# Residual updates and low halves of activations by adding transfers, in a two-layer diffusion step on one Trainium2 core

## The chip, the core and the metric

The kernel runs on one core of one Trainium2 chip. The time is that of the device, in microseconds, for one execution; shown is the median of three runs. Five engines work beside each other, each on its own list of instructions in a fixed order: TensorE (PE in the profile; its weight loads are PEld), VectorE (DVE), ScalarE (ACT), GpSimd (POOL) and SyncE (SP), which here only issues transfers. Data lie in SBUF (128 partitions); products come out in PSUM.

## What is computed

One inference step of a diffusion backbone of two layers. There are 640 tokens: 128 of context and 512 latent ones, which share all weights and differ in their condition vector. Everything is single precision. Cut to what matters:

```python
def swiglu(h, w_in, w_out):                      # w_in 1024 x 5632, w_out 2816 x 1024
    g, u = jnp.split(h @ w_in, 2, axis=-1)
    return (jax.nn.silu(g) * u) @ w_out

def layer(x, cond, p, lam_init, ropes, ctx):
    mods = (jax.nn.silu(cond) @ p['w_ada'] + p['b_ada']).reshape(cond.shape[0], N_MOD, 1, D_MODEL)
    sh1, sc1, g1, sh2, sc2, g2, sh3, sc3, g3 = [mods[:, i] for i in range(N_MOD)]
    h = modulate(rmsnorm(x, p['norm_ffn1']), sh1, sc1)
    x = x + 0.5 * g1 * swiglu(h, p['w_ffn1_in'], p['w_ffn1_out'])
    h = modulate(rmsnorm(x, p['norm_mix']), sh2, sc2)
    y, kv = token_mix(h, p, lam_init, ropes, ctx)
    x = x + g2 * y
    h = modulate(rmsnorm(x, p['norm_ffn2']), sh3, sc3)
    x = x + 0.5 * g3 * swiglu(h, p['w_ffn2_in'], p['w_ffn2_out'])
    return x, kv
```

`token_mix` projects to 2304 columns and mixes in four head groups (pooling, a short convolution, two kinds of attention); its exponentials are those of the attention's softmax.

## The kernel before, in words

**Layout.** Channels lie on the partitions, tokens on the free axis. `x[0]` to `x[7]`, each 128 x 640, hold the residual stream in SBUF for the whole program. Weights are streamed from HBM by SP (`load_raw`, L149) into `raw`, a ring of three buffers of 512 KB that all weights and the ada rows share.

**Single precision from a shorter format.** TensorE's fast format for four-byte numbers (fp32r) keeps fewer bits than single precision. So every operand is held as two: a high half (a copy that rounds, on ScalarE) and a low half (the number less its high half, on VectorE). For weights that is `Weights.piece` (ScalarE `hi` L165, VectorE `lo` L166, 512 columns at a time), for activations `split` (ScalarE L187, VectorE L188). Each product then takes three matmuls: high by high, high by low, low by high.

**Stages.** Two layers of FFN, token mixing, FFN: four FFNs in all. The last FFN has a tail of its own (`last_out`), which also norms and stores the output. A trace of TensorE shows FFN one from 0 to 549 us, mixing to 884, FFN two to 1374, FFN three from 1386 to 1844, mixing to 2166, FFN four to the end.

**An FFN** walks its hidden layer of 2816 in 22 column blocks of 128, in five parts of 5, 5, 4, 4 and 4 blocks (`PARTS`). A part has two stretches:

- The *pair stretch*: `pair(i)` makes gate and up of one block, by a scheme of seven products on the two halves of the tokens in place of eight. It sums weights on VectorE (`f` and `raw`, L602), splits seven pieces of weights, and issues 7 x 12 = 84 matmuls of 322 columns (`product`, L497) into the PSUM banks F, H and S, which ScalarE (L608 and the like) and VectorE take out into `t` tiles. `activation` (L538) then does SiLU on ScalarE, the multiplication on VectorE (L544), and the split (L187, L188).
- The *out stretch*: `out(k0, k1, d, ...)` for eight `d` multiplies the part's activations with the weights of the output (`mm3`, L134; 30 matmuls for a part of five blocks, 24 for one of four) into one of two buffers S, and `x_update_joined` (L518) adds the result, times the gate, to `x[d]`: two VectorE instructions (context columns and latent columns, L522) that read PSUM and `x[d]` and write `x[d]`.

**The ada products.** `mods` of the stages to come are worked out beside the FFNs by the pump: a step (`ada_steps`, L254 to L268) loads 512 KB of `w_ada` into `raw` and multiplies it with two rows on VectorE (`dump`, L264, 128 x 1024 each, with a running sum). `tick` in `activation` and `out` lets the pump go on at a rate for each FFN; in the last FFN there is none. The shift copies `sh` that POOL makes from them are at L375.

**Order and buffers.** The tile framework schedules each engine's instructions into one list from the order of the program and the buffers; there are 38 buffers in ring U (tag "U"; 128 x 644; normed inputs, halves of activations, and in mixing the exponentials `e`), 5 in ring T (`t`), 32 small ones (`s`), 3 in ring F (`f`, in mixing `kx`, which POOL clears at L995). GpSimd makes some low halves in mixing (L166) and small clears; in the FFNs it has nearly nothing to do.

Of the kernel before, what the change touches and what calls it, by code (L numbers as in the profile page):

```python
# [10 lines left out]
F32 = mybir.dt.float32  # L11
# [23 lines left out]
FFN = 2816  # L35
NP = 22
PARTS = ((0, 5), (5, 10), (10, 14), (14, 18), (18, 22))
UB = 38
RAWB = 3
HLB = 4  # L40
NPLAIN = 2
# [40 lines left out]
def hybrid_step(ctx: ExitStack, tc: tile.TileContext, x_in, cc_in, cb_in, w_ada0, w_ada, pv_in, lam_in, w_fin, w_fout, w_min, w_mout,  # L82
# [5 lines left out]
    const = ctx.enter_context(tc.tile_pool(name="const", bufs=1))  # L88
    wp = ctx.enter_context(tc.tile_pool(name="wp", bufs=2))
    up = ctx.enter_context(tc.tile_pool(name="up", bufs=UB))  # L90
    tp = ctx.enter_context(tc.tile_pool(name="tp", bufs=5))
    sp = ctx.enter_context(tc.tile_pool(name="sp", bufs=32))
    psS = ctx.enter_context(tc.tile_pool(name="psS", bufs=2, space=bass.MemoryType.PSUM))
    psH = ctx.enter_context(tc.tile_pool(name="psH", bufs=2, space=bass.MemoryType.PSUM))
    psF = ctx.enter_context(tc.tile_pool(name="psF", bufs=2, space=bass.MemoryType.PSUM))
# [4 lines left out]
    def nm(s):  # L100
        uid[0] += 1
        return f"{s}_{uid[0]}"

    def U(dt=F32R):
        return up.tile([128, UW], dt, tag="U", name=nm("u"))
# [2 lines left out]
        return tp.tile([128, UW], dt, tag="t", name=nm("t"))  # L108

    def E(dt=F32):  # L110
        return up.tile([128, UW], dt, tag="U", name=nm("e"))

    def PT():
        t = up.tile([128, 1024], F32R, tag="P", name=nm("p"), bufs=3)
# [71 lines left out]
    def split(dst_hi, dst_lo, src):  # L186
        S.activation(dst_hi, src, AF.Copy)  # L187
        V.tensor_tensor(out=dst_lo, in0=src, in1=dst_hi, op=ALU.subtract)  # L188
# [329 lines left out]
    def x_update_joined(d, p, gate):  # L518
        g = gate[d // 4]
        w = p.rearrange("p a b -> p (a b)")[:, 512 - HN:512 - HN + N]  # L520
        for c, a, b in SEGS:
            V.scalar_tensor_tensor(out=x[d][:, a:b], in0=w[:, a:b], scalar=g[:, d % 4, c:c + 1], in1=x[d][:, a:b],  # L522
                                   op0=ALU.mult, op1=ALU.add)


    def ffn(l, sub, norm, nxt, pump, prate):
        wi = w_fin[l * 2 + (0 if sub == 0 else 1)]
# [10 lines left out]
        def activation(i, g, u, cb):  # L538

            lb = HW + HN  # L540
            for a, b, c in ((0, NC, cb), (NC, lb, lb)):
                S.activation(g[:, a:b], g[:, a:b], AF.Silu, bias=g[:, c:c + 1])  # L542
            for a, b, c in ((0, NC, cb), (NC, lb, lb)):
                V.scalar_tensor_tensor(out=u[:, a:b], in0=u[:, a:b], scalar=u[:, c:c + 1], in1=g[:, a:b],  # L544
                                       op0=ALU.add, op1=ALU.mult)
            hi, lo = U(), U()
            split(*[t[:, :N].rearrange("p (h n) -> p h n", h=2) for t in (hi, lo)], FastNorm.view(u)[:, :, :HN])
            acts[i] = (hi, lo)
            tick(2.0)

# [88 lines left out]
        def out(k0, k1, d, gate, nx):  # L639
            ps = PS()  # L640
            w = load_w(wo[d, :, k0 * 128:k1 * 128], (k1 - k0) * 128)
            mm3(joined(ps), CN, w, acts[k0:k1], range(k1 - k0))
            x_update_joined(d, ps, gate)
            if nx is not None:
                nx.tile(d)
            tick(1.0)
# [907 lines left out]
```

## Time and profile before

| what | value |
|---|---|
| time, median of 3 runs | 2618.66 us (2615.48 to 2620.7) |
| profiled execution | 2611.82 us |
| its span, first to last instruction | 2610.0 us |
| its mean granted TensorE clock | 0.962 of full speed |
| TensorE / VectorE / ScalarE / POOL busy | 92% / 81% / 46% / 12% of the span |
| moved | 280.63 MB, mean 108 GB/s |

The busy shares are means over the whole program; stages differ. A row of windows gives, all in us where nothing else is said, in this order: the stretch (from:to) and its length; how long PE, PEld, DVE, ACT and POOL were busy, each with its count of instructions in brackets; the clock that TensorE was granted (1.00 is 2.4 GHz, 0.5 is 1.2 GHz); the mean busy share of the sixteen transfer engines; and GB/s. Start times in a timeline overlap a little: an instruction's duration runs to its last write, and the next one starts before that. What one costs its queue is the distance from its start to the start of the next.

### The profile page before, as it was taken

The page shows a single profiled execution, that of the slowest core. Times are in us where ns is not written, and L with a number is a line of the kernel's source. Part 1 is how long each engine was busy: PE and PEld are TensorE (multiplying, and loading weights), DVE is VectorE, ACT ScalarE, POOL GpSimd, SP SyncE. Part 2 cuts the span into 40 slices and gives each one's busy share as a digit, 9 for nine tenths or more (in the row PEclk, how much of TensorE's full clock was granted, in tenths as well). Part 3 has the DMA queues.
Part 4 walks back from the last instruction along what each step waited for, and adds up shares of the span by engine and source line. Part 5 has one row for each costly group of instructions (what it writes and reads, how often), then busy time and mean ns, then how long its engine had stood idle before and what let it go on. Part 6 is the DMA issues. An engine that isn't in the chain of part 4 may idle for free.

```text
span 2610.0 us, 41459 instructions
## 1 busy us (share of the span) xinstructions
PE 2402.5 (92%) x15497; PEld 2318.7 (89%) x15497; DVE 2127.1 (81%) x3978; ACT 1207.9 (46%) x2447; POOL 311.8 (12%) x373
## 2 busy tenths in 40 slices
PE   7798998999788798999998999999998889999998
PEld 4798988998788798988998999999988789999997
DVE  5999998767675899999789898988677768668776
ACT  4533333566554533333355343335575556344444
POOL 3100000034132200000021000001332230000002
PEclk8899999999899899999998999999998999999999
DMA  7254443222412144444322434433233112222223
GB/s 255 92 157 126 149 146 121 77 82 99 146 57 72 61 145 130 154 130 144 96 66 90 137 114 132 134 98 94 71 115 117 58 56 64 89 75 77 77 89 106
DMA packets 100553, 280.63 MB, mean 108 GB/s; under 512 B 10624, under 2 KB 18688, under 8 KB 100352
## 3 DMA queue, kind: packets, MB, share of 16 engines
q1 hardware_dynamic: 100352, 277.99, 33.4%
q8 instruction: 122, 2.00, 0.3%
q14 instruction: 79, 0.65, 0.1%
HBM read 263.00 MB, written 14.94 MB: 106 GB/s over the span
## 4 chain that ended last, share of the span: by engine, by line
PE 56%; DVE 26%; DMA 6%; ACT 6%; issue 4%; POOL 2%; SPq 0%; DVEq 0%; ACTq 0%; POOLq 0%
PE S L134 22%; PE F L497 16%; PE S L497 8%; PE F L134 5%; DVE dump L264 4%; DVE lo L166 4%; PE H L497 3%; DVE u L188 3%; DMA raw<-in_w_ada_dram 2%; DMA raw<-in_w_fin_dram 2%; DVE f L602 2%; PE H L134 2%; ACT hi L165 1%; DVE t L544 1%; DMA u<-qd 1%
## 5 line engine op out<-in xcount | busy, mean ns | idle before, releaser
L134 PE MATMUL S<-u,hi 128*128 128x320 f32 (+3 forms) x3552 | 693.6, 314 | 35.0 <-DVE x L511 16.0
L497 PE MATMUL F<-u,hi 128*128 128x322 f32 x2752 | 643.9, 321 | 57.1 <-ACT hi L165 53.3
L165 ACT ACTIVATE hi<-raw 128x512 fp32r<-128x512 f32 (+2 forms) x696 | 405.2, 594 | 600.9 <-PE S L134 244.9
L134 PEld LDWEIGHTS S<-u,hi 128*128 128x128 f32 x3552 | 566.6, 190 | 49.2 <-issue 18.5
L497 PEld LDWEIGHTS F<-u,hi 128*128 128x128 f32 x2752 | 476.3, 195 | 69.1 <-ACT hi L165 60.9
L166 DVE TENSOR_TENSOR lo<-raw,hi 128x512 fp32r<-128x512 f32 x616 | 392.2, 649 | 82.3 <-ACT hi L165 77.7
L497 PE MATMUL F<-u,lo 128*128 128x322 f32 x1376 | 439.3, 319 | 16.5 <-DVE lo L166 16.4
L134 PE MATMUL S<-u,lo 128*128 128x320 f32 (+3 forms) x1776 | 420.3, 312 | 8.0 <-DVE lo L166 8.0
L264 DVE SCALAR_TENSOR_TENSOR dump<-raw,sc 128x1024 f32<-128x1024 f32 x262 | 321.5, 1231 | 21.5 <-DMA raw<-in_w_ada_dram 17.6
L497 PE MATMUL S<-u,hi 128*128 128x322 f32 x1376 | 323.0, 321 | 7.8 <-DVE t L565 7.8
L134 PEld LDWEIGHTS S<-u,lo 128*128 128x128 f32 x1776 | 303.4, 190 | 10.5 <-DVE lo L166 9.8
L165 ACT ACTIVATE hi<-f 128x512 fp32r<-128x512 f32 x258 | 158.4, 628 | 303.1 <-PE F L497 161.6
L497 PEld LDWEIGHTS F<-u,lo 128*128 128x128 f32 x1376 | 270.9, 197 | 23.1 <-DVE lo L166 22.0
L134 PE MATMUL F<-u,hi 128*128 128x320 f32 (+1 forms) x1056 | 244.7, 321 | 10.0 <-DVE t L762 6.4
L497 PEld LDWEIGHTS S<-u,hi 128*128 128x128 f32 x1376 | 238.7, 195 | 13.0 <-ACT t L608 8.0
L497 PE MATMUL S<-u,lo 128*128 128x322 f32 x688 | 217.4, 316 | 0.0
L166 DVE TENSOR_TENSOR lo<-f,hi 128x512 fp32r<-128x512 f32 x258 | 174.8, 687 | 36.4 <-ACT hi L165 33.9
L522 DVE SCALAR_TENSOR_TENSOR x<-S,gate,x 128x128 f32<-128x128 f32 (+1 forms) x304 | 152.8, 544 | 50.6 <-PE S L134 50.2
L134 PEld LDWEIGHTS F<-u,hi 128*128 128x128 f32 x1056 | 180.5, 194 | 11.9 <-DVE t L762 6.9
L542 ACT ACTIVATE t<-t 128x128 f32<-128x128 f32 (+1 forms) x176 | 98.4, 560 | 140.3 <-DVE t L634 126.9
L134 PE MATMUL F<-u,lo 128*128 128x320 f32 (+1 forms) x528 | 158.6, 318 | 0.0
L497 PE MATMUL H<-u,hi 128*128 128x322 f32 x688 | 156.8, 313 | 1.9 <-ACT hi L165 1.9
(232 smaller groups left out, 3215.9 us busy)
## 6 DMA issues: line engine op xcount, KB each, us to landing
raw<-in_w_fin_dram SPq DMA_DIRECT2D x176, 512.0 KB
raw<-in_w_ada_dram SPq DMA_DIRECT2D x131, 512.0 KB
raw<-in_w_fout_dram SPq DMA_DIRECT2D x104, 256.0 KB
raw<-in_w_fout_dram SPq DMA_DIRECT2D x64, 320.0 KB
raw<-in_w_min_dram SPq DMA_DIRECT2D x36, 512.0 KB
u<-in_w_ada_dram SPq DMA_DIRECT2D x24, 256.0 KB
KS<-kd SPq DMA_DIRECT2D x16, 384.0 KB
raw<-in_w_mout_dram SPq DMA_DIRECT2D x16, 384.0 KB
```

What stands on the lines that cost most here:

```text
L134: PE.matmul(out, lhsT, rhs, start=start, stop=stop)
L165: S.activation(hi[:, :n], src, AF.Copy)
L166: (eng or V).tensor_tensor(out=lo[:, :n], in0=src, in1=hi[:, :n], op=ALU.subtract)
L188: V.tensor_tensor(out=dst_lo, in0=src, in1=dst_hi, op=ALU.subtract)
L264: V.scalar_tensor_tensor(out=dump[:, :D], in0=raw, scalar=1.0, in1=rows[i], op0=ALU.mult, op1=ALU.mult, accum_out=m[0][:, b, i:i + 1])
L497: PE.matmul(ps, w_, a, start=start and k == 0 and p == 0, stop=k == 3 and p == 2, skip_group_check=True)
L522: V.scalar_tensor_tensor(out=x[d][:, a:b], in0=w[:, a:b], scalar=g[:, d % 4, c:c + 1], in1=x[d][:, a:b], op0=ALU.mult, op1=ALU.add)
L542: S.activation(g[:, a:b], g[:, a:b], AF.Silu, bias=g[:, c:c + 1])
L544: V.scalar_tensor_tensor(out=u[:, a:b], in0=u[:, a:b], scalar=u[:, c:c + 1], in1=g[:, a:b], op0=ALU.add, op1=ALU.mult)
L602: V.tensor_tensor(out=o, in0=a, in1=b, op=ALU.add)
```

## The change

`x_update_joined` is replaced by `x_update_dma` in `out` for all parts but the last of each FFN: four parts of eight updates in four FFNs, 128 in all. ScalarE copies the PSUM result, times the gate, into a `t` tile (two instructions), and GpSimd's queue issues a transfer that adds the tile to `x[d]`. The low half of an activation is made by a transfer as well, for all blocks but the last of each part (17 of 22 in an FFN, 68 in all): ScalarE writes the negated high half into `lo`, and a transfer adds the number itself. The exponentials of mixing get a ring of five buffers ("e") of their own, which the low halves use in the FFNs; ring U goes from 38 to 33, ring T from 5 to 6, the small ones from 32 to 16.

```diff
--- before.py
+++ after.py
@@ -35,7 +35,9 @@
 FFN = 2816
 NP = 22
 PARTS = ((0, 5), (5, 10), (10, 14), (14, 18), (18, 22))
-UB = 38
+UB = 33
+EB = 5
+TB = 6
 RAWB = 3
 HLB = 4
 NPLAIN = 2
@@ -88,8 +90,8 @@
     const = ctx.enter_context(tc.tile_pool(name="const", bufs=1))
     wp = ctx.enter_context(tc.tile_pool(name="wp", bufs=2))
     up = ctx.enter_context(tc.tile_pool(name="up", bufs=UB))
-    tp = ctx.enter_context(tc.tile_pool(name="tp", bufs=5))
-    sp = ctx.enter_context(tc.tile_pool(name="sp", bufs=32))
+    tp = ctx.enter_context(tc.tile_pool(name="tp", bufs=TB))
+    sp = ctx.enter_context(tc.tile_pool(name="sp", bufs=16))
     psS = ctx.enter_context(tc.tile_pool(name="psS", bufs=2, space=bass.MemoryType.PSUM))
     psH = ctx.enter_context(tc.tile_pool(name="psH", bufs=2, space=bass.MemoryType.PSUM))
     psF = ctx.enter_context(tc.tile_pool(name="psF", bufs=2, space=bass.MemoryType.PSUM))
@@ -108,7 +110,7 @@
         return tp.tile([128, UW], dt, tag="t", name=nm("t"))
 
     def E(dt=F32):
-        return up.tile([128, UW], dt, tag="U", name=nm("e"))
+        return up.tile([128, UW], dt, tag="e", name=nm("e"), bufs=EB)
 
     def PT():
         t = up.tile([128, 1024], F32R, tag="P", name=nm("p"), bufs=3)
@@ -522,6 +524,15 @@
             V.scalar_tensor_tensor(out=x[d][:, a:b], in0=w[:, a:b], scalar=g[:, d % 4, c:c + 1], in1=x[d][:, a:b],
                                    op0=ALU.mult, op1=ALU.add)
 
+    def x_update_dma(d, p, gate):
+
+        g = gate[d // 4]
+        w = p.rearrange("p a b -> p (a b)")[:, 512 - HN:512 - HN + N]
+        t = T()
+        for c, a, b in SEGS:
+            S.activation(t[:, a:b], w[:, a:b], AF.Copy, scale=g[:, d % 4, c:c + 1])
+        G.dma_start(x[d], t[:, :N], accum_op=ALU.add)
+
 
     def ffn(l, sub, norm, nxt, pump, prate):
         wi = w_fin[l * 2 + (0 if sub == 0 else 1)]
@@ -543,8 +554,14 @@
             for a, b, c in ((0, NC, cb), (NC, lb, lb)):
                 V.scalar_tensor_tensor(out=u[:, a:b], in0=u[:, a:b], scalar=u[:, c:c + 1], in1=g[:, a:b],
                                        op0=ALU.add, op1=ALU.mult)
-            hi, lo = U(), U()
-            split(*[t[:, :N].rearrange("p (h n) -> p h n", h=2) for t in (hi, lo)], FastNorm.view(u)[:, :, :HN])
+            hi, lo = U(), E(F32R)
+            a = FastNorm.view(u)[:, :, :HN]
+            if i + 1 in [k1 for _, k1 in PARTS]:
+                split(*[t[:, :N].rearrange("p (h n) -> p h n", h=2) for t in (hi, lo)], a)
+            else:
+                S.activation(hi[:, :N].rearrange("p (h n) -> p h n", h=2), a, AF.Copy)
+                S.activation(lo[:, :N], hi[:, :N], AF.Copy, scale=-1.0)
+                G.dma_start(lo[:, :N].bitcast(F32).rearrange("p (h n) -> p h n", h=2), a, accum_op=ALU.add)
             acts[i] = (hi, lo)
             tick(2.0)
 
@@ -640,7 +657,7 @@
             ps = PS()
             w = load_w(wo[d, :, k0 * 128:k1 * 128], (k1 - k0) * 128)
             mm3(joined(ps), CN, w, acts[k0:k1], range(k1 - k0))
-            x_update_joined(d, ps, gate)
+            (x_update_dma if k1 < NP else x_update_joined)(d, ps, gate)
             if nx is not None:
                 nx.tile(d)
             tick(1.0)
```

The scheduler places everything anew. In the rows below a line number of the kernel after is up to 17 above that of before for the same code (weight halves L166 become L168, the sums L602 become L619, ada products L264 become L266); L533 is a gate copy of `x_update_dma` and L534 its transfer, L564 the transfer of a low half.

VectorE, first FFN, end of the out stretch of part two and start of the next pair stretch. `x_88` is updated last; `f` and `raw` are sums of weights, `dump` is an ada product. Before:

```order
L522 SCALAR_TENSOR_TENSOR x_84<-S_2689,gate_1254,x_84 128x128
L522 SCALAR_TENSOR_TENSOR x_84<-S_2689,gate_1254,x_84 128x512
L166 TENSOR_TENSOR lo_2811<-raw_2781,hi_2810 128x512
L602 TENSOR_TENSOR f_2786<-raw_2781,raw_2783 128x512
L264 SCALAR_TENSOR_TENSOR dump_2929,mod_2926<-raw_2927,sc_315 128x1024
L602 TENSOR_TENSOR raw_2783<-raw_2783 128x512
L264 SCALAR_TENSOR_TENSOR dump_2929,mod_2926<-raw_2927,sc_318 128x1024
L522 SCALAR_TENSOR_TENSOR x_88<-S_2738,gate_1256,x_88 128x128
L522 SCALAR_TENSOR_TENSOR x_88<-S_2738,gate_1256,x_88 128x512
L602 TENSOR_TENSOR f_2785<-raw_2783,raw_2781 128x512
L602 TENSOR_TENSOR f_2787<-f_2785,raw_2781 128x512
L166 TENSOR_TENSOR lo_2831<-f_2785,hi_2830 128x512
```

After:

```order
L619 TENSOR_TENSOR f_2826<-raw_2821,raw_2823 128x512
L619 TENSOR_TENSOR raw_2823<-raw_2823 128x512
L619 TENSOR_TENSOR f_2825<-raw_2823,raw_2821 128x512
L168 TENSOR_TENSOR lo_2834<-raw_2821,hi_2833 128x512
L619 TENSOR_TENSOR f_2827<-f_2825,raw_2821 128x512
L168 TENSOR_TENSOR lo_2851<-raw_2821,hi_2850 128x512
L266 SCALAR_TENSOR_TENSOR dump_2970,mod_2967<-raw_2968,sc_315 128x1024
L266 SCALAR_TENSOR_TENSOR dump_2970,mod_2967<-raw_2968,sc_318 128x1024
L168 TENSOR_TENSOR lo_2871<-f_2825,hi_2870 128x512
L266 SCALAR_TENSOR_TENSOR dump_2975,mod_2967<-raw_2973,sc_315 128x1024
L168 TENSOR_TENSOR lo_2888<-f_2826,hi_2887 128x512
```

The last two updates of `x` stood between the weight sums before; now no update is there, and the four sums come close together, ahead of the ada products.

ScalarE at the same place; `t_2791` and `t_2831` take the first product out of bank F, a `t` from `S` and a gate is a copy of an x update. Before:

```order
L165 ACTIVATE hi_2793<-raw_2781 128x512
L165 ACTIVATE hi_2810<-raw_2781 128x512
L608 ACTIVATE t_2791<-F_2788 128x322
L165 ACTIVATE hi_2830<-f_2785 128x512
L165 ACTIVATE hi_2847<-f_2786 128x512
L165 ACTIVATE hi_2865<-raw_2783 128x512
L165 ACTIVATE hi_2882<-raw_2783 128x512
L165 ACTIVATE hi_2899<-f_2787 128x512
```

After:

```order
L167 ACTIVATE hi_2833<-raw_2821 128x512
L167 ACTIVATE hi_2850<-raw_2821 128x512
L533 ACTIVATE t_2766<-S_2725,gate_1258 128x128
L533 ACTIVATE t_2766<-S_2725,gate_1258 128x512
L167 ACTIVATE hi_2870<-f_2825 128x512
L167 ACTIVATE hi_2887<-f_2826 128x512
L533 ACTIVATE t_2817<-S_2776,gate_1260 128x128
L533 ACTIVATE t_2817<-S_2776,gate_1260 128x512
L167 ACTIVATE hi_2905<-raw_2823 128x512
L625 ACTIVATE t_2831<-F_2828 128x322
L167 ACTIVATE hi_2922<-raw_2823 128x512
L167 ACTIVATE hi_2939<-f_2827 128x512
```

Four gate copies of the last two updates stand between the high halves of the first pair's weights, and the copy out of bank F comes after two more halves and two gate copies.

POOL, first FFN, around the last part. Before, with the shift copies of the next stages:

```order
L375 COPY sh_8876<-mod_4148 128x4x2
L376 COPY sh_8876<-mod_4148 128x4
L377 COPY sh_8876<-mod_4148 128x4
L995 MEMSET kx_5570 64x128
L995 MEMSET kx_5571 64x128
L349 MEMSET R_5683 128x2
L330 COPY u_5196<-shc_5202 128x2
```

After:

```order
L534 DMA x_88<-t_4653 128x640
L564 DMA e_4799<-t_4668 128x2x320
L564 DMA e_4945<-t_4814 128x2x320
L1012 MEMSET kx_5651 64x128
L1012 MEMSET kx_5652 64x128
L564 DMA e_5091<-t_4960 128x2x320
L351 MEMSET R_5764 128x2
L332 COPY u_5277<-shc_5283 128x2
```

The clears of `kx` stood behind shift copies; now transfers stand ahead of them and one low half of the last part stands behind them.

## Rows read from the trace of the kernel before

**Rows 1.** The page, part 1: busy time, share of the span, instructions, per engine.

```profile
PE 2402.5 (92%) x15497; PEld 2318.7 (89%) x15497; DVE 2127.1 (81%) x3978; ACT 1207.9 (46%) x2447; POOL 311.8 (12%) x373
```

**Rows 2.** Windows: a pair stretch and an out stretch, last FFN.

```profile
2258.00:2321.00 63.00, 63.00 (x422) 62.54 (x421) 54.25 (x95) 33.83 (x63) 0.00 (x0) 1.00 0.24 75
2321.00:2357.00 36.00, 35.85 (x245) 35.59 (x245) 19.36 (x39) 9.60 (x19) 0.00 (x0) 1.00 0.32 94
```

**Rows 3.** Windows: four of the eleven pair stretches of FFNs one to three.

```profile
170.00:245.00 75.00, 67.38 (x419) 65.80 (x418) 69.43 (x129) 32.40 (x64) 0.00 (x0) 0.93 0.35 111
283.00:338.00 55.00, 51.05 (x335) 49.45 (x334) 54.57 (x99) 25.46 (x49) 0.00 (x0) 1.00 0.38 120
370.00:437.00 67.00, 57.25 (x339) 55.58 (x339) 61.24 (x110) 27.13 (x52) 1.48 (x9) 0.90 0.36 117
...
1592.00:1646.00 54.00, 51.93 (x343) 50.68 (x342) 52.48 (x97) 25.82 (x49) 1.86 (x6) 1.00 0.37 119
```

**Rows 4.** Windows: four out stretches of FFNs one and two.

```profile
245.00:283.00 38.00, 36.41 (x243) 35.41 (x242) 34.54 (x70) 8.64 (x19) 0.00 (x0) 1.00 0.58 184
338.00:370.00 32.00, 29.42 (x194) 28.26 (x194) 29.49 (x58) 6.53 (x11) 0.00 (x0) 1.00 0.60 192
1064.00:1102.00 38.00, 36.67 (x245) 35.69 (x244) 34.46 (x71) 8.44 (x18) 1.00 (x3) 1.00 0.59 184
1159.00:1191.00 32.00, 29.49 (x194) 28.32 (x194) 29.69 (x59) 6.71 (x11) 0.00 (x0) 1.00 0.61 193
```

**Rows 5.** Waits: who waited for whom, us in total, times, longest us.

```profile
ACT hi L165 <- DVE f L602: 69.2, 28, 5.3
...
PE F L497 <- ACT hi L165: 53.3, 23, 3.8
...
PE F L497 <- DVE lo L166: 16.4, 14, 1.6
```

**Rows 6.** Timeline of VectorE: start us, us, engine, line, operation, tiles.

```profile
290.05 1.22 DVE L264 SCALAR_TENSOR_TENSOR dump<-raw,sc 128x1024 f32<-128x1024 f32 x1
291.20 0.08 DVE L264 DVE_READ_ACCUMULATOR dump<-raw,sc 128x1 f32 x1
...
391.13 0.82 DVE L188 TENSOR_TENSOR u<-t,u 128x640 fp32r<-128x640 f32 x1
391.87 0.68 DVE L602 TENSOR_TENSOR f<-raw,raw 128x512 f32<-128x512 f32 x1
```

**Rows 7.** Timeline of VectorE: the last x update of part two, first FFN.

```profile
283.62 1.00 DVE L522 SCALAR_TENSOR_TENSOR x<-S,gate,x 128x128 f32<-128x128 f32 x2
284.54 0.68 DVE L602 TENSOR_TENSOR f<-raw,raw 128x512 f32<-128x512 f32 x1
```

**Rows 8.** Groups by form, ScalarE: count | busy, mean ns | idle before, releasers.

```profile
L187 ACT ACTIVATE u<-t 128x640 fp32r<-128x640 f32 x88 | 64.9, 737 | 27.4 <-DVE t L544 27.1
...
L187 ACT ACTIVATE p<-S 128x512 fp32r<-128x512 f32 x64 | 38.2, 597 | 46.2 <-PE H L134 29.8 <-DVE p L188 12.9 <-PE S L946 2.5
```

**Rows 9.** Waits of POOL.

```profile
POOL sh L375 <- DVE mod L267: 777.8, 6, 315.5
...
POOL kx L995 <- DVE lo L166: 153.8, 4, 82.8
```

**Rows 10.** Timeline: two weight loads issued by SP's queue, and ScalarE after them.

```profile
338.65 2.07 SPq L151 DMA_DIRECT2D raw<-in_w_fout_dram  x2
...
342.12 0.63 ACT L165 ACTIVATE hi<-raw 128x512 fp32r<-128x512 f32 x1 [2.27 <-DMA raw<-in_w_fout_dram]
```

**Rows 11.** The page, part 3: the loads' queue: packets, MB, share of sixteen engines.

```profile
q1 hardware_dynamic: 100352, 277.99, 33.4%
```

**Rows 12.** Groups by form: operations with two SBUF operands, VectorE and POOL.

```profile
L264 DVE SCALAR_TENSOR_TENSOR dump<-raw,sc 128x1024 f32<-128x1024 f32 x262 | 321.5, 1231 | 21.5 <-DMA raw<-in_w_ada_dram 17.6 <-ACT sc L247 2.6
...
L166 POOL TENSOR_TENSOR lo<-raw,hi 128x512 fp32r<-128x512 f32 x64 | 87.8, 1374 | 271.2 <-ACT hi L165 238.8 <-ACT e L1196 20.2 <-ACT e L937 6.1
...
L322 DVE SCALAR_TENSOR_TENSOR u<-x,scl,u 128x512 fp32r<-128x512 f32 x16 | 24.0, 1500 | 9.2 <-ACT u L321 9.2
```

## Prediction

> **What bounds the kernel now.** I read the page first. TensorE is busy for 2402.5 of 2610 us and VectorE for 2127.1 [rows 1], so TensorE looks like the limit; but both figures are means over stages with different limits. So I cut the span into the stretches of the program. An FFN is five parts, and a part is a *pair stretch* (4 or 5 column blocks of the hidden layer, 84 matmuls each) and an *out stretch* (8 output blocks of 30 or 24 matmuls).
>
> The last FFN has no ada products, and there TensorE is full: a pair stretch does 422 matmuls in 63.0 us and an out stretch 245 in 36.0 us [rows 2]. That is 0.149 and 0.147 us a matmul, and serves as the yardstick. VectorE is busy there for 54.25 of 63 us.
>
> The same stretches of the first three FFNs are longer [rows 3]. The pair stretch at 370 us does 339 matmuls in 67.0 us where the yardstick gives 50.6: 16.4 us lost. VectorE lists 61.24 us of work, and the granted clock falls to 0.90, which it does where TensorE has stood still. Eleven such stretches lose between 2.8 us (the one at 1592) and 16.4 us, 101 us in all. Four out stretches lose 2.0 to 3.5 us, 11.3 us together [rows 4]; VectorE is busy there for 29.49 of 32.0 us or 34.54 of 38. The waits of TensorE name ScalarE's weight halves (53.3 us) and VectorE's (16.4 us) [rows 5], and ScalarE's halves wait for sums that VectorE makes. So in the first three FFNs VectorE's queue sets the end of a pair stretch; the ada products (1.15 us each, from the start to the read of its sum [rows 6]) are what fills it.
>
> **The change part by part.** Durations come from the profiled execution (2611.82 us, its span 2610.0); the median of the three runs shown is 2618.66, 6.84 us more.
>
> *Low halves.* 17 of 22 per FFN leave VectorE. One takes 0.74 us from its start to the next start [rows 6]. Only where VectorE is the limit does that count: 4 in each of the parts with five blocks, 3 in those with four. That is 3.0 or 2.2 us a stretch.
>
> *x updates.* 32 per FFN leave VectorE, 0.92 us each (two instructions, 283.62 to 284.54 [rows 7]). In an out stretch TensorE sets the pace, so most of it is hidden. Two things are not. The four out stretches of [rows 4] are short of VectorE by at most 3.5 us and get 8 x 0.92 = 7.4 us back: all 11.3 us go. And the last update of a part waits for the last matmul of its out stretch, with the first sums of the next pair stretch queued behind it (the row at 284.54 is such a sum). In the order as printed above nothing of VectorE's stands between them any more: 0.92 us for each pair stretch that follows such an out stretch.
>
> *Ada products.* Without the work above, the scheduler puts the products elsewhere. Counted in VectorE's order, pair stretches two, three and four of the first FFN hold 15, 12 and 13 of them before and 14, 10 and 11 now. In the second FFN stretches one to four go 15 to 16, 15 to 14, 12 to 10 and 13 to 11; in the third FFN only the second changes, 9 to 8. Each that moves to an out stretch is worth 1.15 us [rows 6].
>
> *Sum over the pair stretches*, in order of time and never more than a stretch loses. First FFN: 3.0 + 1.15 + 0.92 = 5.1; 2.2 + 2.3 + 0.92 = 5.4, held at its loss of 5.0 (the stretch at 283 [rows 3]); 5.4. Second: 3.0 - 1.15 = 1.8 (the mixing before it keeps its updates on VectorE); 5.1; 5.4; 5.4. Third: 3.0; 5.1; 2.8 (held); 3.1. Together 47.2, and 3.0 for the first stretch of the program, which is short of VectorE too: 50.2 us. With the out stretches 61.5 us.
>
> *What it costs.* ScalarE gets a negating copy per low half (nearest row 737 ns) and two copies per x update (nearest 597 ns from PSUM for the long one [rows 8]). In the stretch at 370 ScalarE works 27.13 of 67 us [rows 3]. If idle time covers all, it costs nothing; if each of the 38 negating copies in the eleven stretches delays a weight half, 28 us. I take 5, since a copy can delay a half only in the few places where TensorE already waits for ScalarE (23 waits [rows 5]). At the start of a pair stretch the last update's two copies stand between weight halves (second order above); the next evacuation of bank F then comes after five instructions of ScalarE and before the third product, which starts 24 x 0.149 = 3.6 us in; I put it at nothing. Cover gone, it costs some 0.5 us a stretch.
>
> POOL issues 196 transfers, and is a queue: in the last part of the FFNs before a mixing, the third low half stands behind two clears of `kx` (third order above), and `kx` waits up to 82.8 us for VectorE [rows 9]. They are released within the last pair, so this half may start only near the end of the pair stretch and is wanted 14 matmuls, 2.1 us, into the out stretch. Nearest landing: a 256 KB load issued by 340.72 lets ScalarE go on at 342.12, some 1.4 us [rows 10]. Between 0 and 4 us in each of two places; I take 1 each. The other low halves have a pair (84 x 0.149 = 12.5 us) to land. POOL's copies of ada shifts, which wait up to 315.5 us for VectorE [rows 9], stand ahead of some adds too; in VectorE's new order what they wait for is done within the same pair stretch as before, so I price that at nothing.
>
> Transfer engines: the loads take 33.4% of 2610 us for 277.99 MB [rows 11], 3.1 us of all sixteen per MB. An added transfer of 0.328 MB is then 1.03 us if it costs one copy, and up to 3.1 if it costs three. I take one copy: in the fullest out stretch (share 0.60 of 32 us [rows 4]) 19.2 + 8.2 = 27.4 us, less than TensorE's 28.5. It is hidden.
>
> Mixing: the exponentials' own five buffers change TensorE's order of scores and projections a little and VectorE's work not at all. I take 0, between -10 and +10. The last FFN gains nothing: TensorE is full there.
>
> Net 61.5 - 5 - 2 = 54.5 us: 2557 us for an execution like the profiled one, **2564 us** for the median.
>
> **The rivals.**
> *All of the loss goes.* A stretch with VectorE at 0.95 also pays for the half clock behind each stop. If VectorE's slack ends the stops altogether, the 101 + 11.3 us go and about 5 of cost stay: 2512 us. For it: the loss at 370 is three times what I credit. Against it: my counts leave 2 to 7 us more VectorE work in four of the stretches than TensorE needs.
>
> *The transfer engines fill up in the out stretches.* If an add must read the old value as well, it costs two copies, 2.06 us. Then the two stretches with four blocks and ada loads need 19.2 + 16.5 = 35.7 against 28.5 us, and four with five blocks 22.4 + 16.5 = 38.9 against 36 (share 0.59 of 38 [rows 4]): at most 26 us back, 2590 us. For it: the share of 0.60. Against: the updates have a whole part to land, and can spill into the pair stretch with its share of 0.36.
> The Trainium skill, "Collectives: The Full Stack", section "The bandwidth ceiling: the fold count and why AG ≠ RS ≠ AR", says of adds done by the DMA engines that they read two sources and so push twice the read traffic. By that rule this rival's 2.06 us would be the price; no row here shows an adding transfer.
>
> *Slower: issuing on POOL holds VectorE.* VectorE's operations with two operands in SBUF stretch when POOL works beside them: 1500 ns for 512 columns against 1231 ns for 1024 [rows 12]. If the issue of a transfer holds VectorE for h, a low half gains 0.74 - h and an update 0.92 - h. At h = 0.85 nothing is left; that is the point from which it decides. At the 1374 ns of a POOL subtraction [rows 12] the 38 low halves add 24 us and six full out stretches 6 x 8 x (1.374 - 0.92) = 22, less 11.5 for the moved products, plus 7: +41, **2660 us**.
> The Trainium skill, "SBUF — State Buffer", section "Who interferes with whom", has a VectorE instruction with two SBUF inputs contend with a GpSimd instruction that reads SBUF, not with one that only writes. By it the 1500 ns row is explained, and whether an issue counts as reading no run here shows.
>
> That the change does not do what it says is excluded by the order: 128 updates and 68 subtractions are gone from VectorE.
>
> **How the numbers follow.** My forecast 0.52 (its own range 2540 to 2590: costs of 0 to 28 us on ScalarE, mixing 10 either way), all of the loss 0.15, full transfer engines 0.18, POOL holding VectorE 0.15. About 0.2%, 5 us, is what a measurement of this kernel can tell from no change. Faster: nearly all of the first three, 0.78. No change: the last rival near h = 0.85 and the tails, 0.07. Slower: 0.15. The range 2512 to 2624 takes the first three cases and the mild end of the last, and leaves out less than 2 in 10.
>
> **What would show it.** Right: the pair stretch at 370 some 5 us shorter and its granted clock higher; the out stretches of [rows 4] at 0.147 us a matmul; VectorE's busy time lower by 68 x 0.82 + 128 x 1.0, some 180 us; the last FFN unchanged. Wrong: VectorE's subtractions and ada products longer than now beside POOL's issues; weight loads landing later in out stretches, with ScalarE waiting for them; TensorE waiting for ScalarE in the last FFN; longer mixing.

## The result, and the profile after

The changed kernel takes 2574.15 us (median of 4 runs, 2566.68 to 2574.75) against 2619.65 us of the kernel before beside it (4 runs): a ratio of 0.9823, 95% interval 0.9801 to 0.9844. The forecast was 2564 us, range 2512 to 2624. The time agrees; the reasons do not. The profile shows nearly all of the gain where the forecast put nothing.

The profiled execution of the kernel after takes 2574.67 us (span 2572.9). The windows cut both spans at the ends of the two mixing stretches of TensorE (some 1300 matmuls each). The rows are of the kernel before, with the columns as told ahead of the prediction:

```profile
0.00:594.00 594.00, 538.61 (x3352) 507.41 (x3353) 500.15 (x936) 252.19 (x499) 61.51 (x100) 0.95 0.42 134
594.00:822.00 228.00, 198.43 (x1305) 187.62 (x1304) 159.78 (x323) 134.47 (x307) 70.54 (x77) 0.94 0.28 94
822.00:1886.00 1064.00, 991.22 (x6393) 968.00 (x6391) 928.08 (x1708) 458.79 (x901) 74.71 (x89) 0.97 0.36 112
1886.00:2108.00 222.00, 195.28 (x1301) 184.96 (x1301) 158.89 (x323) 132.26 (x305) 71.43 (x77) 0.95 0.26 90
2108.00:2610.00 502.00, 478.97 (x3154) 470.75 (x3152) 380.19 (x692) 230.18 (x440) 33.62 (x34) 0.98 0.26 80
```

The same of the kernel after:

```profile
0.00:593.00 593.00, 542.40 (x3350) 508.70 (x3351) 460.14 (x854) 289.88 (x581) 105.00 (x148) 0.95 0.58 162
593.00:793.00 200.00, 190.03 (x1306) 181.56 (x1305) 154.05 (x323) 135.02 (x305) 68.93 (x77) 0.98 0.31 104
793.00:1866.00 1073.00, 988.75 (x6391) 962.13 (x6391) 849.06 (x1546) 534.16 (x1064) 172.60 (x186) 0.97 0.53 142
1866.00:2067.00 201.00, 190.36 (x1305) 181.54 (x1304) 153.86 (x323) 133.44 (x303) 69.45 (x77) 0.98 0.29 97
2067.00:2572.00 505.00, 478.81 (x3154) 470.53 (x3152) 340.67 (x611) 267.36 (x521) 83.05 (x83) 0.97 0.45 112
```

The two mixing stretches are 28 and 21 us shorter. The stretches with the FFNs in them, where all the adding transfers are, are 1 us shorter, 9 us longer and 3 us longer. And yet VectorE did what was forecast there: 500.15 to 460.14 us and 928.08 to 849.06 us of work. So VectorE was relieved and TensorE did not get the time.

The next windows are of the kernel after. The first four answer to [rows 3] and [rows 4], in the first FFN; the last two answer to [rows 2]:

```profile
243.00:281.00 38.00, 36.29 (x245) 35.41 (x243) 25.75 (x52) 14.51 (x33) 6.04 (x7) 1.00 0.84 221
281.00:342.00 61.00, 53.80 (x336) 51.22 (x335) 55.21 (x100) 28.64 (x54) 4.46 (x4) 0.97 0.53 146
342.00:375.00 33.00, 30.33 (x196) 29.81 (x195) 23.85 (x44) 13.24 (x25) 5.21 (x6) 0.95 0.84 219
375.00:436.00 61.00, 55.10 (x335) 52.52 (x334) 55.68 (x101) 28.72 (x55) 6.99 (x14) 0.94 0.57 153
...
2222.00:2285.00 63.00, 63.00 (x423) 62.48 (x422) 50.61 (x89) 36.82 (x70) 5.66 (x5) 1.00 0.43 104
2285.00:2321.00 36.00, 35.96 (x246) 35.70 (x246) 13.14 (x25) 16.03 (x33) 6.03 (x7) 1.00 0.64 153
```

In the out stretch at 243 VectorE is down to 25.75 of 38 us, and the stretch is as long as before (38.00 for 245 matmuls where it was 38.00 for 243). What has gone up is the share of the transfer engines: 0.58 to 0.84. The pair stretch that began at 370 is 6 us shorter, the one that began at 283 is 6 us longer. The last FFN is as before. Now the waits (who waited for whom, us in total, times, longest us); first two of the kernel before, then the kernel after:

```profile
DVE dump L264 <- DMA raw<-in_w_ada_dram: 17.6, 25, 2.1
...
DVE f L602 <- DMA raw<-in_w_fin_dram: 7.6, 10, 1.5
```

```profile
DVE f L619 <- DMA raw<-in_w_fin_dram: 75.4, 40, 5.5
DVE dump L266 <- DMA raw<-in_w_ada_dram: 72.9, 41, 5.2
...
PE F L499 <- ACT hi L167: 29.8, 11, 7.1
...
POOL kx L1012 <- DVE lo L168: 17.0, 4, 6.8
...
PE F L499 <- ACT t L625: 15.5, 11, 3.8
PE F L499 <- DVE lo L168: 14.7, 21, 2.1
```

VectorE now stands and waits for loads: 75.4 us for weights in place of 7.6, 72.9 us for ada rows in place of 17.6. A new wait of TensorE is that for `t` out of bank F, 15.5 us in 11 places. The page's part on queues (packets, MB, share of the sixteen transfer engines) tells what the adds cost the engines that also carry the loads:

```profile
q1 hardware_dynamic: 100352, 277.99, 33.6%
q0 software_dynamic: 36928, 64.24, 15.1%
```

15.1% of 2572.9 us is 388.5 us of all sixteen engines for 196 adds: 1.98 us each, 6.0 us a MB. A load costs 33.6% for 277.99 MB, 3.1 us a MB. An add costs two copies. That does not come from shorter packets: among the trace's packets of 2560 bytes, one of an x update takes 215 ns by the median and one of a load 102 ns.

So there are two theories for the runs. **A:** the exponentials' own buffers, which free mixing, are the gain. **B:** VectorE's relief is the gain, as recorded ahead, and mixing gained by it too. For the FFNs there are two more: **C**, the adds' bytes delay loads and take back what VectorE won, or **D**, the new order of VectorE does.

### The profile page after: what moved, and what is told of

Read it like the earlier page. It is cut to its first block, busy times and chain, and to the rows that moved or that the text cites. A ratio compares the mean times of both kernels' runs of the same rounds, so it can differ in the third digit from the quotient of the medians.

```text
span 2572.9 us, 42089 instructions
## 1 busy us (share of the span) xinstructions
PE 2390.3 (93%) x15497; PEld 2304.5 (90%) x15497; DVE 1957.8 (76%) x3654; ACT 1359.9 (53%) x2771; POOL 499.0 (19%) x569
## 3 DMA queue, kind: packets, MB, share of 16 engines
q1 hardware_dynamic: 100352, 277.99, 33.6%
q0 software_dynamic: 36928, 64.24, 15.1%
## 5 line engine op out<-in xcount | busy, mean ns | idle before, releaser
L499 PE MATMUL F<-u,hi 128*128 128x322 f32 x2752 | 638.4, 319 | 54.6 <-ACT hi L167 29.8
L499 PEld LDWEIGHTS F<-u,hi 128*128 128x128 f32 x2752 | 470.4, 193 | 68.5 <-ACT hi L167 33.4
L136 PE MATMUL S<-u,hi 128*128 128x320 f32 (+3 forms) x2144 | 485.0, 317 | 40.6 <-DVE x L513 21.9
L168 DVE TENSOR_TENSOR lo<-raw,hi 128x512 fp32r<-128x512 f32 x616 | 390.7, 647 | 154.5 <-ACT hi L167 149.6
L136 PEld LDWEIGHTS S<-u,hi 128*128 128x128 f32 x2144 | 361.1, 193 | 52.4 <-issue 23.0
L266 DVE SCALAR_TENSOR_TENSOR dump<-raw,sc 128x1024 f32<-128x1024 f32 x262 | 321.4, 1232 | 76.8 <-DMA raw<-in_w_ada_dram 72.9
L136 PE MATMUL S<-e,hi 128*128 128x320 f32 (+2 forms) x1408 | 329.2, 311 | 1.5 <-DVE e L190 1.3
L499 PEld LDWEIGHTS S<-u,hi 128*128 128x128 f32 x1376 | 239.7, 196 | 14.0 <-ACT t L640 11.0
L564 POOL DMA_DIRECT2D e<-t x68 | 82.0, 1206 | 873.7 <-DVE t L633 198.6
L136 PEld LDWEIGHTS S<-e,hi 128*128 128x128 f32 x1408 | 237.0, 189 | 4.1 <-DVE e L190 3.2
L136 PE MATMUL F<-u,hi 128*128 128x320 f32 (+1 forms) x1056 | 238.8, 318 | 0.8 <-DVE x L513 0.3
L534 POOL DMA_DIRECT2D x<-t x128 | 110.4, 863 | 582.3 <-ACT t L533 577.8
L168 DVE TENSOR_TENSOR lo<-f,hi 128x512 fp32r<-128x512 f32 x258 | 175.7, 687 | 48.3 <-ACT hi L167 46.1
L136 PEld LDWEIGHTS F<-u,hi 128*128 128x128 f32 x1056 | 178.4, 193 | 3.0 <-DVE x L513 0.9
```

Source lines behind the costliest of these rows:

```text
L136: PE.matmul(out, lhsT, rhs, start=start, stop=stop)
L168: (eng or V).tensor_tensor(out=lo[:, :n], in0=src, in1=hi[:, :n], op=ALU.subtract)
L266: V.scalar_tensor_tensor(out=dump[:, :D], in0=raw, scalar=1.0, in1=rows[i], op0=ALU.mult, op1=ALU.mult, accum_out=m[0][:, b, i:i + 1])
L499: PE.matmul(ps, w_, a, start=start and k == 0 and p == 0, stop=k == 3 and p == 2, skip_group_check=True)
L534: G.dma_start(x[d], t[:, :N], accum_op=ALU.add)
L564: G.dma_start(lo[:, :N].bitcast(F32).rearrange("p (h n) -> p h n", h=2), a, accum_op=ALU.add)
```

## The experiments

**E1: the rings without the adds.** Edit of the kernel after:

```diff
-            (x_update_dma if k1 < NP else x_update_joined)(d, ps, gate)
+            x_update_joined(d, ps, gate)
-            if i + 1 in [k1 for _, k1 in PARTS]:
+            if True:
```

> The changed kernel's rings (U 33, exponentials 5 of their own, T 6, small ones 16), but every x update on VectorE again and every low half made there: no adding transfer. Theory A (the 45 us come from the two mixing stretches, whose TensorE went from 228 and 222 us to 200 and 201 us because the exponentials no longer take buffers of ring U; the FFNs gain nothing net): 2565 to 2580 us, both mixing stretches at about 200 us. Theory B (the working on record: the gain is VectorE's relief in the FFNs, the rings are worth nothing): 2610 to 2625 us.

2582.87 us, ratio to before 0.9843 (0.9827 to 0.986). Nearly the whole gain is there with no adding transfer. The time lies just outside A's range; B falls.

**E2: the exponentials' ring alone**, T at 5 and the small ones at 32. Edit of the kernel before:

```diff
-UB = 38
+UB = 33
-        return up.tile([128, UW], dt, tag="U", name=nm("e"))
+        return up.tile([128, UW], dt, tag="e", name=nm("e"), bufs=5)
-            hi, lo = U(), U()
+            hi, lo = U(), E(F32R)
```

> The kernel before with one thing changed: the exponentials (and, in the FFNs, the low halves of activations) have five buffers of their own and ring U has 33; T stays 5, the small ones 32, no adding transfer. Theory A: all of the mixing gain is here, 2565 to 2580 us. Rival A2 (a sixth T buffer is what frees mixing): at most a third of it, 2600 us or more. Theory B: 2610 to 2625 us.

2573.66 us, ratio 0.9807 (0.9792 to 0.9821): as fast as the whole change. A holds, A2 falls. T at 6 and 16 small ones did not help but cost 9.2 us between E1 and E2 (the intervals do not touch); why was not tried. The two mixing stretches in E2, 26 and 23 us shorter than in the kernel before:

```profile
594.00:796.00 202.00, 192.00 (x1308) 183.42 (x1307) 154.13 (x323) 135.27 (x306) 69.36 (x77) 0.97 0.32 103
...
1870.00:2069.00 199.00, 187.06 (x1302) 178.03 (x1301) 153.47 (x322) 133.10 (x303) 68.94 (x77) 1.00 0.29 98
```

What mixing waited for shows best in the longest wait of TensorE that goes away. TensorE's waits, SP's waits and SP's queue, kernel before:

```profile
PE H L134 <- DMA u<-qd: 11.6, 3, 9.1
...
SPq L181 <- ACT u L801: 10.7, 2, 9.3
```

```profile
632.99 1.75 SPq L1122 DMA_DIRECT2D qd<-t  x2
645.11 0.65 SPq L181 DMA_DIRECT2D KS<-kd  x1
...
659.80 3.99 SPq L181 DMA_DIRECT2D u<-qd  x3
```

SP's queue in E2:

```profile
631.84 1.39 SPq L1122 DMA_DIRECT2D qd<-t  x2
...
643.94 1.17 SPq L181 DMA_DIRECT2D u<-qd  x2
```

Queries of the differential heads are stored at 633 and read back into buffers of ring U. Before, the reading back was issued at 659.80, 27 us after the store, and TensorE stood for it for up to 9.1 us; in E2 it goes out after 12 us and no such wait is left. In the kernel before, two windows of mixing have a lower granted clock, 0.88 from 640 to 680 and 0.87 from 760 to 800, and TensorE is busy there for 29.57 and 32.94 of 40 us; in E2 the first is at 1.00 (the lowest window of E2's first mixing stretch is 0.91, from 720 to 760):

```profile
640.00:680.00 40.00, 29.57 (x199) 27.63 (x198) 21.48 (x49) 20.92 (x50) 7.06 (x13) 0.88 0.40 135
...
760.00:800.00 40.00, 32.94 (x195) 30.88 (x193) 27.32 (x58) 21.10 (x49) 12.94 (x10) 0.87 0.10 30
```

```profile
640.00:680.00 40.00, 39.10 (x277) 37.10 (x276) 33.23 (x74) 27.27 (x65) 8.04 (x7) 1.00 0.42 143
```

That the ring is the cause is shown; by what path is not. SP issues in the order of its list. Ahead of the queries it had stood 9.3 us for pooling's work on ScalarE (L801) before it reloaded keys at 645.11. Those keys go into ring KS, which they share with pooling and whose size no run changed. In E2 the same work of pooling is over by 616 us and the keys are reloaded at 619.88. This speaks for a new order of mixing as a whole more than for one buffer of ring U that was held too long, but it was not tried. And the 11.6 us of this wait are only a part of the 49 us that the two stretches gain.

**E3: the adds with the rings of before.** It is the kernel after with U 38, `e` in ring U, T 5 and 32 small ones.

> The rings of the kernel before (U 38 with the exponentials in it, T 5, small ones 32), with both kinds of adding transfers. Theory A: mixing stays at 220 to 230 us of TensorE, and the time is that of before or a little more, 2610 to 2630 us. Theory B: 2565 to 2580 us.

2617.23 us (10 runs), ratio 0.9979 (0.9965 to 0.9993). A holds; TensorE stands for `u<-qd` for 11.6 us again. All 196 adds together bring 0.2%.

**E4: adds of one column.** It leaves out all but the first column of each addition (of each half of the tokens in a low half). Edit of the kernel after:

```diff
-        G.dma_start(x[d], t[:, :N], accum_op=ALU.add)
+        G.dma_start(x[d][:, :1], t[:, :1], accum_op=ALU.add)
```

and the low halves' transfer likewise.

> The changed kernel, but each adding transfer moves only the first column (per half of the tokens) of its tile: as many instructions, issues and waits, next to no bytes. It leaves out the rest of each addition. Theory C (in the FFNs what VectorE won is lost because the adds fill the transfer engines in the out stretches, 0.84 to 0.86 of them, and weight and ada loads land late): FFNs one to three get 20 to 40 us shorter, 2535 to 2555 us. Theory D (not the bytes, but the new order of VectorE and the three raw buffers, held by ada products at the head of a pair stretch): 2565 to 2577 us.

2512.9 us, ratio 0.9577 (0.9561 to 0.9592). The bytes cost 61 us, more than C said; D falls. It is not that an engine stands for the adds themselves: in the change only VectorE does, for 2.3 us in all. And the number of packets is the same, as the queue's row shows, so it is not their count:

```profile
q0 software_dynamic: 36928, 0.15, 2.3%
```

The pair, out and pair stretch that answer to 281 to 436 above are 55, 32 and 54 us long where they were 61, 33 and 61, and VectorE's waits for loads are shorter than the change's 75.4 and 72.9 us:

```profile
270.00:325.00 55.00, 51.11 (x335) 49.48 (x335) 51.84 (x94) 27.36 (x51) 3.93 (x4) 1.00 0.46 127
325.00:357.00 32.00, 29.65 (x201) 29.03 (x200) 26.59 (x48) 14.50 (x30) 6.35 (x8) 1.00 0.65 183
357.00:411.00 54.00, 50.95 (x334) 49.30 (x333) 52.76 (x98) 27.57 (x52) 6.49 (x13) 1.00 0.47 132
```

```profile
DVE dump L266 <- DMA raw<-in_w_ada_dram: 47.1, 39, 3.0
DVE f L619 <- DMA raw<-in_w_fin_dram: 42.0, 28, 5.0
```

Two things have to be kept apart here. The two waits add up to 25 us before, 89 in E4 and 148 in the change. The first step comes without bytes, so it does not tell of late loads: a VectorE with less to do may just come to a load earlier. Only the second, 59 us, is the bytes'. That loads land later with it can be worked out from the landings in the traces: a weight load of 512 KB for gate and up takes 3.6 us from issue to landing in E2 and in E4, and 4.2 in the change, by the median; one in ten takes more than 4.6, 4.7 and 6.0 us. ScalarE's waits for weight loads are 83 us in E4 and 139 in the change.

The sums of whole stretches tell where the time goes. Each is taken from its first matmul to the first of the next stretch, in the FFNs one to three; the eleven pair stretches are those of the prediction. E7 and E9 follow below.

| us | before | E2 | change | E4 | E7 | E9 |
|---|---|---|---|---|---|---|
| eleven pair stretches | 706.8 | 715.9 | 708.5 | 656.7 | 708.0 | 682.2 |
| twelve out stretches | 394.8 | 395.9 | 402.1 | 393.9 | 406.8 | 391.9 |
| of these the four of [rows 4] | 139.3 | 140.5 | 139.4 | 135.9 | 142.7 | 134.0 |

The FFNs of E2 run the same operations as those of the kernel before, so their 9 us in the first row tell how far two traces can differ (that of the kernel before is of an execution of 2611.82 us, 12 under the median beside E2). Of the 60 us by which these stretches are longer in the change than in E4, 52 lie in the pair stretches, where the share of the transfer engines is 0.53 and 0.57 in the two shown, and 8 in the out stretches.

**E5 to E7: low halves alone, x updates alone, both**, each with E2's rings. E5 has the x updates on VectorE and E6 the low halves, each by one of the two edits shown at E1; E7 is the kernel after with T 5 and 32 small ones.

> The exponentials' own ring (T 5, small ones 32, as in the run with that ring alone, 2573.7 us) with only the 68 low halves by adding transfers; x updates on VectorE. Theory C (the bytes of the adds take back what VectorE wins, where the loads need the transfer engines, in the out stretches above all): the low halves move in pair stretches, with a share of 0.38 before, so most of their gain stays: 2545 to 2565 us. Rival C2 (any added byte delays the loads, wherever it moves): 2570 to 2577 us.

> The same rings with only the 128 x updates by adding transfers; low halves on VectorE. Theory C: the updates move in the out stretches, where the loads need the engines, so they lose what they win: 2570 to 2585 us. Rival C2: their share of the 64 MB is 65%, and so is their share of the gain: within 3 us of the ring alone, 2570 to 2577 us. Rival C3 (updates are what gains, low halves lose): 2550 to 2562 us.

> The changed kernel with T back at 5 and the small ones at 32. The run of all rings without adds was 9 us slower than the exponentials' ring alone; if T 6 and 16 small ones cost that here too, 2560 to 2568 us; if the adds need the sixth T buffer (ScalarE's copies hold one until the transfer has read it), 2575 us or more.

E5: 2547.44 us, 0.9712 (0.9691 to 0.9733). E6: 2592.08 us, 0.9884 (0.9866 to 0.9902). E7: 2571.54 us, 0.9805 (0.9787 to 0.9822), between its two expectations: the adds do not need the sixth T buffer, and against the change's 0.9823 nothing more can be told. Against the ring alone (2573.7) the low halves win 26 us, the updates lose 18. C2 and C3 fall. C holds for the low halves; the updates lost more than it allowed.

**E8: low halves on POOL.** E5 with, in place of the negating copy and the transfer,

```diff
+                G.tensor_tensor(out=lo[:, :N].rearrange("p (h n) -> p h n", h=2), in0=a, in1=hi[:, :N].rearrange("p (h n) -> p h n", h=2), op=ALU.subtract)
```

> The same rings, x updates on VectorE, and the 68 low halves by a subtraction on POOL: no added byte, and no negating copy on ScalarE. If POOL reading SBUF holds up VectorE's operations with two SBUF operands, those lengthen in the FFNs (sums L619 and weight halves L168 above 690 ns) and the time is 2573 us or more. If it doesn't, VectorE is relieved without bytes and it is 2540 to 2560 us.

2577.32 us, 0.9826 (0.981 to 0.9841): nothing won over the ring alone. First the busy times of the engines, in E2 and then in E8; then groups by form, one of the kernel before and three of E8:

```profile
PE 2393.4 (93%) x15497; PEld 2311.7 (90%) x15497; DVE 2114.9 (82%) x3978; ACT 1209.1 (47%) x2447; POOL 308.3 (12%) x373
PE 2394.6 (93%) x15497; PEld 2309.9 (90%) x15497; DVE 2124.9 (83%) x3910; ACT 1210.6 (47%) x2447; POOL 441.1 (17%) x441
```

```profile
L166 DVE TENSOR_TENSOR lo<-raw,hi 128x512 fp32r<-128x512 f32 x552 | 376.0, 691 | 82.3 <-ACT hi L165 77.7 <-PE H L917 2.1
```

```profile
L168 DVE TENSOR_TENSOR lo<-raw,hi 128x512 fp32r<-128x512 f32 x552 | 392.1, 719 | 72.3 <-ACT hi L167 67.2 <-PE H L933 2.1
...
L266 DVE SCALAR_TENSOR_TENSOR dump<-raw,sc 128x1024 f32<-128x1024 f32 x262 | 330.7, 1267 | 34.2 <-DMA raw<-in_w_ada_dram 30.9 <-ACT sc L249 2.6
...
L563 POOL TENSOR_TENSOR e<-t,u 128x640 fp32r<-128x640 f32 x68 | 137.9, 2028 | 1441.2 <-ACT u L562 1067.1 <-issue 177.6 <-PE H L499 131.6
```

While POOL reads two operands of SBUF, VectorE's operations with two are held up: by the mean, 28 ns on each of 552 weight halves and 36 ns on each of 262 products, 25 us together. The sums of weights add 22 us (the 86 in place go from 701 ns in E2 to 890). In all, the 68 subtractions that left VectorE (56 us busy, 68 x 0.82) took nothing off its busy time: it is 2124.9 us, where E2 has 2114.9. With VectorE as busy as before there was nothing to win.

**E9: whole low halves, x updates of one column** (E7 with the edit shown at E4).

> The kernel with both kinds of adds and T 5 (2571.5 us), but each x update's transfer adds only the first column; the low halves are whole. It leaves out the rest of each x update. Theory C (it is the updates' bytes, in the out stretches, that cost): 2508 to 2522 us, near the run in which all adds had one column (2512.9). Rival C2 (bytes cost alike wherever they move): the low halves' third of the bytes costs some 20 us, 2530 to 2540 us. Rival C4 (the updates cost by ScalarE's copies or the T buffers, not by bytes): 2560 us or more.

2529.39 us, 0.9639 (0.9623 to 0.9656). C falls in its strict form (only the updates' bytes cost), C4 too. It is the range of this run's C2 but for 0.6 us: bytes cost alike wherever they move (the C2 of E5 went further and had them cost all that the low halves win). The updates' 41.95 MB cost 42 us (E7 less E9). The low halves' 22.29 MB cost 16 us (E9 less E4), or 19 to 26 if the T and small rings of E4 slow it as much as they did the change against E7 (2.6) or E1 against E2 (9.2). A MB costs 1.0 us in one place and 0.7 to 1.2 in the other; what differs is what stands against it. And the updates' bytes, which are issued in the out stretches, cost the pair stretches some 26 us and the out stretches some 15 (E7 and E9 in the table above).

**E10: updates on POOL.** It is E7 with `G.tensor_tensor(out=x[d], in0=t[:, :N], in1=x[d], op=ALU.add)` for the updates' transfer.

> Low halves by adding transfers as before; for an x update ScalarE's two scaled copies stay, and POOL adds the tile to x in one operation: no bytes. The out stretches of FFNs one to three had VectorE nearly full, and with low halves on POOL VectorE's weight halves went from 691 to 719 ns on average. If holding up VectorE costs less than the bytes and the updates: 2515 to 2545 us, faster than low halves alone (2547.4). If it costs as much as it saves: 2545 to 2560 us.

2568.15 us, 0.9785 (0.9766 to 0.9804), 21 us slower than low halves alone. Both expectations fall. POOL's add takes 1791 ns, VectorE's products go to 1306 ns, and VectorE is busy for 2048.4 us where E7, with the same operations on it, has 1954.7:

```profile
L266 DVE SCALAR_TENSOR_TENSOR dump<-raw,sc 128x1024 f32<-128x1024 f32 x262 | 340.8, 1306 | 35.6 <-DMA raw<-in_w_ada_dram 31.8 <-ACT sc L249 2.6
L534 POOL TENSOR_TENSOR x<-t,x 128x640 f32<-128x640 f32 x128 | 228.9, 1791 | 482.6 <-ACT t L533 482.6
```

**E11 and E12: two of eight updates by adds**, the last two of each part, or the first two (E7 with `and d in ORDER[-2:]`, or `ORDER[:2]`, behind `k1 < NP`).

> Low halves by adding transfers, and of each part's eight x updates only the last two, a quarter of the updates' bytes. The last updates are those that stand ahead of the next pair stretch's sums in VectorE's order (0.92 us each). If that queueing is most of what an update is worth, 2530 to 2545 us; if the updates' gain is VectorE's time as such, it and the bytes cancel and the time is that of low halves alone, 2545 to 2552 us.

> As the run with the last two x updates of each part by adding transfers (2540.0 us), but the first two instead: as many bytes and as much of VectorE's time saved, at the other end of the out stretch. If what counts is that the last updates stand ahead of the next pair stretch's sums, this wins nothing over low halves alone, or loses the bytes: 2547 to 2558 us. If it is VectorE's time as such, 2537 to 2545 us.

E11: 2539.95 us, 0.9683 (0.966 to 0.9706). E12: 2544.9 us, 0.9715 (0.9699 to 0.9731). E12 is where low halves alone are (0.9712), E11 a little below. That speaks for the place of the last updates in VectorE's queue, but the intervals overlap, so it stays open. E11 is the fastest kernel here that leaves nothing out, by the medians: 3.2% under the kernel before, and 34 us under the change.

## Why the prediction came out, step by step

Here is a chain of medians, each run to the next: the kernel before 2623.5 (beside E1 to E4), exponentials' ring 2573.7 (**-49.8**), low halves with their bytes 2547.4 (**-26.2**), updates without their bytes 2529.4 (**-18.1**), the updates' bytes 2571.5 (**+42.2**), T 6 and 16 small ones 2574.2 (+2.6, within the spread). The low halves' -26.2 is a relief of some 43 us less bytes of some 16 (45 to 52 less 19 to 26 by the larger prices at E9).

- *What bounds the kernel* was right: VectorE's queue set the pair stretches, and taking work off it without adding bytes shortens them (E4).
- *The sum of 61.5 us* for VectorE's relief agrees in total with the 18 + 43 = 61 us of the runs (63 to 70 by the larger prices), but the runs have ScalarE's and POOL's costs in them already, so that the forecast to hold beside them is the net 54.5. The parts agree less. Without bytes (E4) the eleven pair stretches are 50 us shorter than before and 59 shorter than in E2, where 47.2 were forecast. The four out stretches of [rows 4] are 3 to 5 us shorter, where "all 11.3 us" were to go. That term of the updates fails even without bytes: most of what TensorE loses in those out stretches is not the updates' doing, and what else it is was not tried.
- *"I take one copy ... It is hidden"* is the step that failed. The price of an add was 1.98 us and not 1.03, and it was not hidden: it cost about 60 us. The rival named the price (2.06 us) but not the place: it took only what overflows an out stretch, at most 26 us, and 52 of the 60 us were lost in the pair stretches. There need be no overflow: the engines were at 0.84 in the out stretches, not at 1, and at 0.53 in a pair stretch, and loads came late all the same. The waits for them (59 us more on VectorE, 56 more on ScalarE than in E4) fit a chain in which each late load holds up what stands behind it in these queues; that chain is argued and was not tried by itself.
  The Trainium skill, "Collectives: The Full Stack", section "The bandwidth ceiling: the fold count and why AG ≠ RS ≠ AR", has the adding step of a ReduceScatter read two sources and so push twice the read traffic of a copy; this case's queue rows agree (6.0 against 3.1 us a MB).
- *"Mixing: ... I take 0, between -10 and +10"* failed as well, by 50 us to the other side. The two errors, +60 and -50, cancel; that 2564 was near 2574 is luck. The change of the order of scores and projections was seen, and no wait of mixing was priced: TensorE's row on `u<-qd` was in the trace.
- *ScalarE's cost*, 5 us: no run takes it by itself, and it is not where it was put. TensorE waits less for ScalarE's weight halves (53.3 to 29.8 us), while the copy out of bank F, priced at nothing, now holds TensorE for 15.5 us. It does so with whole x updates (11.4 us in E6), less with one-column ones (8.2 in E9, 1.1 in E4), and hardly without (1.3 in E2 and in E5). VectorE waits too: its weight halves stand 195.8 us for ScalarE's, where it was 111.6 before and 111.9 in E5.
- *Issuing on POOL holds VectorE* is excluded by the rows of the kernel after:

```profile
L266 DVE SCALAR_TENSOR_TENSOR dump<-raw,sc 128x1024 f32<-128x1024 f32 x262 | 321.4, 1232 | 76.8 <-DMA raw<-in_w_ada_dram 72.9 <-ACT sc L249 2.6
...
L534 POOL DMA_DIRECT2D x<-t x128 | 110.4, 863 | 582.3 <-ACT t L533 577.8 <-issue 4.5
...
L564 POOL DMA_DIRECT2D e<-t x68 | 82.0, 1206 | 873.7 <-DVE t L633 198.6 <-DVE raw L619 176.5 <-DVE dump L266 164.6
```

  An issue takes POOL 863 or 1206 ns, and the ada product takes 1232 ns where it took 1231 [rows 12]. POOL's arithmetic is another matter (E8, E10).
  The Trainium skill, "SBUF — State Buffer", section "Who interferes with whom", puts it so that a VectorE instruction with two SBUF inputs contends with a GpSimd instruction that reads SBUF. E8 and E10 agree (products 1267 and 1306 ns); the issues of adding transfers left the products at 1232 ns.
- *POOL as a queue*: `kx` waits 6.8 us at the longest where it waited 82.8 [rows 9]; no loss shows there.
- *All of the loss goes*, 2512 us: E4's 2512.9 meets the number without the bytes, and by another sum. 50 us of it are the ring's, in mixing, and of the 101 us that the pair stretches lost only some 50 to 59 came back.
- *What would show it*: the stretch at 370 did get 6 us shorter and its clock went from 0.90 to 0.94, VectorE's work fell by 169 us (180 forecast), the last FFN did not change. The out stretches of [rows 4] at 0.147 us a matmul did not come. Of the signs against, weight loads landing later came true, but ScalarE does not wait for them longer than before (139 us, 146 before); it is VectorE that does. Mixing became shorter, not longer.

## What to carry to other kernels

A transfer that adds is not free because its queue is empty: price it as two copies on the engines that bring the weights, and ask which loads are then late; here they were late at a share of 0.53. When a change also repartitions buffer rings, read the waits of the stage that uses the ring, even if the change seems to be about another, and run the rings by themselves. A total that agrees proves nothing of its terms: here two errors of 50 and 60 us hid each other until each part was run alone.

## What the hardware showed that was not expected

An adding transfer of 320 KB within SBUF keeps all sixteen engines for 1.98 us by the mean (2.3 us a low half, whose packets are half as long, and 1.84 an x update, by the queue rows of E5 and E6). It lands 4.9 us (low halves) or 5.4 us (x updates) after its issue, by the median. One column, 1.0 or 0.5 KB, still takes 3.1 or 3.6 us (E4):

```profile
x<-t POOLq DMA_DIRECT2D x128, 320.0 KB, 5.4
...
e<-t POOLq DMA_DIRECT2D x68, 320.0 KB, 4.9
```

At a mean share of 0.5 to 0.6 in a pair stretch, added bytes cost 0.7 to 1.2 us of the kernel's time per MB.

Sixty-eight subtractions moved to POOL left VectorE's busy time where it was (2124.9 us in E8, 2114.9 in E2): what they took off it came back in its other operations, for the most part those with two operands in SBUF.
